# Three modulation vectors of layer 0 as rows on TensorE, and all 31 convolution taps of layer 0 on VectorE

## The chip, the cores and the metric

The kernel runs on one core of one Trainium2 chip. The metric is the device time of one execution in microseconds (us). One execution was taken by the profiler, and all rows shown here come from it. PE is TensorE (matmuls), DVE is VectorE, ACT is ScalarE, POOL is GpSimd, and SP is the engine that issues most of the DMAs. SPq, ACTq and POOLq are the sequencers that issue DMAs.

## What is computed

Two streams of 256 tokens of width 1024, `ctx` and `x`, go through two layers of a first block; then `x` alone goes through a second block. Only the first layer is touched by the change. Cut to what matters there (both streams run it, each with its own modulation vector):

```python
mod = split(silu(c) @ w_mod[l] + b_mod[l], 6)        # x;  the same weights with silu(c_ctx) for ctx
shift1, scale1, gate1, shift2, scale2, gate2 = mod   # parts 0, 1, 2, 3, 4, 5, each 1024 long
xn = rms_norm(x, g1) * (1 + scale1) + shift1
p = xn @ w_in                                        # q, k, v, fourier, conv, pool columns
attn = attend(q, k, v)
four = fft2(p_f).real @ w_f
glu = p_c[:256] * sigmoid(p_c[256:])
y = depthwise_conv(glu, dw_w, width 31) + dw_b       # 256 channels
conv = silu(layer_norm(y)) @ w_pw
mix = concat(attn, four, conv, pool) @ w_out
x = x + gate1 * mix
xn = rms_norm(x, g2) * (1 + scale2) + shift2
x = x + gate2 * swiglu(xn)
```

Part 2 is therefore needed after `@ w_out`, parts 3 and 4 at the second norm, part 5 at the end of the layer.

## The kernel before

Activations are kept feature by token: 128 features on the partitions, 512 columns, of which 256 belong to each stream (`x` is s=0, `ctx` is s=1). A large product is split into three products of rounded high and low halves (`mm3` at L270, `tm` at L283): a weight half of 512 KB is loaded by SP into the ring `raw` of 4, ACT writes its high part `wh` (L241) and DVE, seldom POOL, the low part `wl` (L243). The ring of `wh`, `wl` also has 4 buffers.

The program's text is written as generators on `Flow` (L114), a small clock of estimated times: `tick` advances it with each product, `spawn` starts a side job, `yield d` gives up for d estimated us, and `join` waits for a job. This only sets in which order instructions are written. The order on PE, DVE, ACT and POOL is then made by a scheduler; each engine runs its own list strictly in that order. SP's list is as written.

**Startup** (L479 to L485, `LOADS = "mhmhmm"`). SP loads `XC` (the input, four times 512 KB), then in turn weights of modulation (`m`, `mod_pair`) and of the first projection (`h`). `mod_pair(g)` (L437) makes a quarter of parts 0 and 1 of layer 0 on PE. silu(c) of both streams lies in `scf` as 32 columns (2 used) for each of 8 blocks k of 128 inputs. The array is used as four groups of 32 columns: for each k four matmuls with the same small weights `scf[:, k]` and four different sets of 128 weight columns write four groups of 32 partitions of one PSUM tile `p_mod`. ACT copies it to SBUF, one transpose on PE (`p_modt`) turns rows to columns, and DVE adds the bias. `in0_k` (L464) then norms block k and issues 12 products of the projection `p_c` (the two convolution halves). At the end `scb_fill` (L367) spreads silu(c) over all partitions by 16 transposes (`p_scb`).

**Side job `mod_bg`** (L390) makes all other modulation vectors, ten parts (those of layer 0 in the order 2, 4, 3, 5). For each block of 128 outputs ACT issues a load of 512 KB into a tile `wm` of four (after a one-column copy on POOL, L398, which ties it to the progress of other work), and DVE multiplies it by the spread silu(c) and sums along the row: once for ctx (L403, result tile `jg`) and once for x (L405, written over `wm`). It begins when both convolutions are written.

**Mixer of layer 0.** After `p_c` come q and k, v (`p_q`, `p_kv`), fourier and pool columns. The convolution of each of two channel tiles f has 31 taps: taps 0 to 7 on PE as products with diagonal matrices (`conv_diag` L551 writes them on ACT, `conv_pe` L559 multiplies into `p_cv`), taps 8 to 30 on DVE as one multiply-add each over 512 columns (`conv_taps`, L567 and L571), then `p_cv` is added (L575). `conv_ln` (L582) follows: mean by PE (`p_mean`), subtraction on DVE (L591), squares on ACT (L593), `p_var`, the root on POOL (`rs_r`, L297), its spread by PE (`p_lnr`), multiplication on DVE (L606), silu on ACT (L607), and the product `p_pw` (L614). Attention runs first for s=1, then for s=0: per unit `p_s` (PE), minimum (DVE), exponential (ACT), transposes (PE), copy `pT` (ACT), `p_o` (PE). The output projection `p_wo` of 512 columns runs over k = 0 to 3 (fourier, pool), 6 and 7 (convolution), 4 and 5 (attention) for m = 0 to 3, then for m = 4 to 7 stream by stream. `update` adds gate1 (part 2) times it to `XC`; then comes the second norm (`norm_mod`), whose normed blocks `AH`, `AL` feed `p_ua`.

Of the kernel before, what the change touches and what calls it, by code (L numbers as in the profile page):

```python
# [24 lines left out]
F32 = mybir.dt.float32  # L25
# [3 lines left out]
OP = mybir.AluOpType  # L29
AX = mybir.AxisListType  # L30

D = 1024
KT = 8
T = 256
NF = 22
EPS = 1e-6
TAPS = 31
# [7 lines left out]
LOADS = "mhmhmm"  # L45
NPE = 8
CVD, FOD = 0.9, 1
# [104 lines left out]
@with_exitstack  # L152
def tile_kernel(ctx, tc, xin, pk_d, rows_d, lc_d, bc_d, wmod0, wmod, win, wout, wfi, wfo, wsm, win2, wproj, wout2,
                wgu, wdn, wst, pos, out, dump=None):
    nc = tc.nc
# [35 lines left out]
    def P(name, i=0, n=1):  # L191
        return pk[:, PK[name] + i:PK[name] + i + n]
# [197 lines left out]
    def mod_bg(parts, *deps):  # L390

        yield from wait(*deps)
        for l, part, with_ctx, gap_ in parts:
# [20 lines left out]
            mods.add((l, part))  # L414

# [83 lines left out]
    for l in range(2):  # L501
# [4 lines left out]
        with ExitStack() as mctx:  # L506
# [40 lines left out]
            def conv_diag(f):  # L547

                w = lpool.tile([128, D], F32, tag="wm", name="cdg", bufs=WMB)
                for j in range(NPE):  # L550
                    S.activation(w[:, 128 * j:128 * j + 128], ident, AF.Copy,  # L551
                                 scale=pk[:, PK[f"dw_{l}"] + f * TAPS + j:PK[f"dw_{l}"] + f * TAPS + j + 1])
                return w

            def conv_pe(f, w):

                cps[f] = psm("p_cv")
                for j in range(NPE):
                    PE.matmul(cps[f][:, :N].rearrange("p (s t) -> p s t", t=T), w[:, 128 * j:128 * j + 128],  # L559
                              GP[:, f, :, j:j + T], start=j == 0, stop=j == NPE - 1)  # L560
                    tick(0.0017 * N)

            def conv_taps(f, delay):
                y = Y[:, f].rearrange("p (s t) -> p s t", t=T)
                dw = PK[f"dw_{l}"] + f * TAPS
                per = 0.35 * ns
                V.tensor_scalar(y, GP[:, f, :, NPE:NPE + T], pk[:, dw + NPE:dw + NPE + 1], P(f"db_{l}", f), op0=OP.mult,  # L567
                                op1=OP.add)
                yield per + delay
                for j in range(NPE + 1, TAPS):  # L570
                    V.scalar_tensor_tensor(y, GP[:, f, :, j:j + T], pk[:, dw + j:dw + j + 1], y, op0=OP.mult, op1=OP.add)  # L571
                    yield per + delay
                while f not in cps:
                    yield 0.3
                V.tensor_tensor(Y[:, f], cps[f][:, :N], Y[:, f], op=OP.add)  # L575
                yield per
                G.tensor_copy(snap, Y[:, f, 0:1])
# [224 lines left out]

            cdg = [conv_diag(f) for f in range(2)]
            if l == 1:
# [21 lines left out]
            if l == 0:  # L826
                spawn(mod_bg([(0, 2, True, BG0), (0, 4, True, BG0), (0, 3, True, BG0), (0, 5, True, BG1),
                              (1, 1, True, BG1), (1, 0, True, BG1), (1, 2, False, BG1), (1, 4, False, BG1),
                              (1, 3, False, BG1), (1, 5, False, BG1)], cv0, cv1))
            for s in streams[::-1]:  # L830
# [15 lines left out]
            done(n_, 3)  # L846
            for f in range(2):
                conv_pe(f, cdg[f])
            at = []
# [535 lines left out]
def _pack(inp):  # L1385
    inp = {k: np.asarray(v) for k, v in inp.items()}
    a = {}
# [64 lines left out]

_ORDER = ["xin", "pk", "rows", "lc", "bc", "wmod0", "wmod", "win", "wout", "wfi", "wfo", "wsm", "win2", "wproj", "wout2",
          "wgu", "wdn", "wst", "pos"]
# [18 lines left out]
```

## Time and profile before

| | |
|---|---|
| median of 3 runs | 1367.46 us (1367.43 to 1368.42) |
| the profiled execution | 1368.16 us, span in the trace 1366.5 us |
| mean granted TensorE clock | 0.994 of full |
| DMA | 223.79 MB, mean 164 GB/s |

The span is the time from the first to the last instruction in the trace; the execution's own time is 1.7 us longer. In rows of instructions the columns are start, duration, engine, line, operation, output<-inputs, shape, number of instructions that follow one another (xN), and in brackets the idle time of that engine before it with what ended it. A matmul leaves two records here where its operands are full 32-bit numbers, so four matmuls of a modulation step are eight records.

### The profile page before, as it was taken

How to read it: one execution, taken by the hardware profiler on the slowest of the kernel's cores; microseconds unless marked ns; L12 is line 12 of the kernel's file. 1: busy time of each engine (PE TensorE's matmuls, PEld its weight loads, DVE VectorE, ACT ScalarE, POOL GpSimd, SP SyncE). 2: the span in 40 equal slices, each digit the busy share in tenths (PEclk: the TensorE clock that was granted, in tenths of full speed). 3: DMA queues.
4: the chain of work that ended last, by engine and by line, in shares of the span. 5: the costliest groups of instructions: out<-in, count | busy, mean ns of one | idle time of the engine just before them, and what ended most of it. 6: DMA issues, size and time to landing. Idle time of an engine off the chain costs nothing.

```text
span 1366.5 us, 23461 instructions
## 1 busy us (share of the span) xinstructions
PE 1329.0 (97%) x9220; PEld 1193.9 (87%) x9220; DVE 893.6 (65%) x1572; ACT 608.3 (45%) x1016; POOL 262.1 (19%) x295
## 2 busy tenths in 40 slices
PE   5999999899999999999999999999999999999997
PEld 3886569788888888899799999999999999999997
DVE  4597998999873333369577666665655657655554
ACT  5434534323232222244655554455655555544452
POOL 1034634143310000123330000110200003222211
PEclk9999999999999999999999999999999999999998
DMA  9424452687973222333145555665335344545463
GB/s 367 181 77 137 141 170 95 230 262 259 318 254 108 93 83 76 105 133 135 47 145 180 185 176 162 193 244 171 108 120 175 109 145 169 192 168 176 157 203 105
DMA packets 66478, 223.79 MB, mean 164 GB/s; under 512 B 7488, under 2 KB 8640, under 8 KB 66368
## 3 DMA queue, kind: packets, MB, share of 16 engines
q1 hardware_dynamic: 53824, 178.16, 38.9%
q10 hardware_dynamic: 12080, 42.50, 9.1%
q8 instruction: 72, 1.18, 0.4%
q0 software_dynamic: 464, 1.64, 0.3%
q14 instruction: 38, 0.31, 0.1%
HBM read 221.22 MB, written 1.05 MB: 163 GB/s over the span
## 4 chain that ended last, share of the span: by engine, by line
PE 90%; DVE 4%; POOL 2%; ACT 1%; DMA 1%; issue 1%; SPq 0%; POOLq 0%; DVEq 0%; ACTq 0%
PE p_dn L271 6%; PE p_dn L273 6%; PE p_dn L272 6%; PE p_ua L272 5%; PE p_ua L273 5%; PE p_ua L271 5%; PE p_ug L272 5%; PE p_ug L273 5%; PE p_ug L271 4%; PE p_wo L271 2%; PE p_wo L272 2%; PE p_wo L273 2%; PE p_bq L287 2%; PE p_bq L289 2%; PE p_bq L288 2%; PE p_ga L273 2%
## 5 line engine op out<-in xcount | busy, mean ns | idle before, releaser
L243 DVE TENSOR_TENSOR wl<-raw,wh 128x1024 fp32r<-128x1024 f32 (+2 forms) x340 | 388.6, 1145 | 279.0 <-ACT wh L241 277.8
L241 ACT CAST wh<-raw 128x1024 fp32r<-128x1024 f32 (+1 forms) x344 | 332.1, 973 | 296.9 <-PE p_dn L272 91.8
L273 PE MATMUL p_dn<-HH,wl 128*128 128x256 f32 (+1 forms) x550 | 171.7, 312 | 0.5 <-DVE wl L243 0.5
L271 PE MATMUL p_dn<-HH,wh 128*128 128x256 f32 (+1 forms) x550 | 172.0, 313 | 0.0
L272 PE MATMUL p_dn<-HL,wh 128*128 128x256 f32 (+1 forms) x550 | 171.6, 312 | 0.0
L313 POOL TENSOR_TENSOR ss<-ss,sq 128x256 f32<-128x256 f32 (+1 forms) x43 | 49.3, 1145 | 438.0 <-ACT sq L312 292.0
L272 PE MATMUL p_ua<-AL,wh 128*128 128x258 f32 (+2 forms) x368 | 122.9, 334 | 3.7 <-DVE AL L339 3.7
L273 PE MATMUL p_ua<-AH,wl 128*128 128x258 f32 (+2 forms) x368 | 122.8, 334 | 0.0
L273 PE MATMUL p_ug<-AH,wl 128*128 128x258 f32 (+2 forms) x368 | 122.3, 332 | 0.0
L271 PE MATMUL p_ua<-AH,wh 128*128 128x258 f32 (+2 forms) x368 | 122.1, 333 | 0.0
L272 PE MATMUL p_ug<-AL,wh 128*128 128x258 f32 (+2 forms) x368 | 122.0, 331 | 0.0
L271 PE MATMUL p_ug<-AH,wh 128*128 128x258 f32 (+2 forms) x368 | 121.6, 331 | 0.0
L273 PEld LDWEIGHTS p_dn<-HH,wl 128*128 128x128 f32 x550 | 104.3, 190 | 6.7 <-DVE wl L243 0.7
L272 PEld LDWEIGHTS p_dn<-HL,wh 128*128 128x128 f32 x550 | 104.3, 190 | 6.1
L271 PEld LDWEIGHTS p_dn<-HH,wh 128*128 128x128 f32 x550 | 104.3, 190 | 6.2 <-ACT wh L241 0.2
L405 DVE SCALAR_TENSOR_TENSOR wm<-wm,scb 128x1024 f32<-128x1024 f32 x80 | 99.0, 1242 | 10.1 <-DMA wm<-in_wmod 9.9
L272 PEld LDWEIGHTS p_ua<-AL,wh 128*128 128x128 f32 x368 | 69.7, 189 | 11.3 <-DVE AL L339 4.1
L273 PEld LDWEIGHTS p_ua<-AH,wl 128*128 128x128 f32 x368 | 69.9, 190 | 7.1
L271 PEld LDWEIGHTS p_ua<-AH,wh 128*128 128x128 f32 x368 | 69.8, 190 | 7.2
L272 PEld LDWEIGHTS p_ug<-AL,wh 128*128 128x128 f32 x368 | 69.5, 189 | 7.2
L273 PEld LDWEIGHTS p_ug<-AH,wl 128*128 128x128 f32 x368 | 69.4, 189 | 6.9
L271 PEld LDWEIGHTS p_ug<-AH,wh 128*128 128x128 f32 x368 | 69.3, 188 | 7.0
(367 smaller groups left out, 3329.4 us busy)
## 6 DMA issues: line engine op xcount, KB each, us to landing
raw<-in_wfi SPq DMA_DIRECT2D x88, 512.0 KB, 3.7
raw<-in_win SPq DMA_DIRECT2D x84, 512.0 KB, 3.9
wm<-in_wmod ACTq DMA_DIRECT2D x80, 512.0 KB, 4.5
raw<-in_wgu SPq DMA_DIRECT2D x44, 512.0 KB, 3.7
raw<-in_wout SPq DMA_DIRECT2D x24, 512.0 KB, 3.6
raw<-in_wfo SPq DMA_DIRECT2D x32, 384.0 KB, 3.1
raw<-in_wfo SPq DMA_DIRECT2D x32, 320.0 KB, 3.2
rawm<-in_wmod SPq DMA_DIRECT2D x16, 512.0 KB, 10.1
```

The costliest lines, as they stand in the source:

```text
L241: S.copy(h[:, :n], raw[:, :n])
L243: (G if every and j % every == 0 else V).tensor_tensor(lo[:, :n], raw[:, :n], h[:, :n].bitcast(F32), op=OP.subtract)
L271: PE.matmul(ps, w[0], a[0], start=first, stop=False, **kw)
L272: PE.matmul(ps, w[0], a[1], start=False, stop=False, **kw)
L273: PE.matmul(ps, w[1], a[0], start=False, stop=last, **kw)
L287: PE.matmul(ps, a[0], w[0], start=k == 0, stop=False)
L288: PE.matmul(ps, a[0], w[1], start=False, stop=False)
L289: PE.matmul(ps, a[1], w[0], start=False, stop=k == KT - 1)
L313: (eng or G).tensor_tensor(ss[0][:, cs], ss[0][:, cs], sq[:, :n], op=OP.add)
L405: V.scalar_tensor_tensor(w, w, 1.0, scb[:, 0], op0=OP.mult, op1=OP.mult, accum_out=modv[:, l, part, 0, k:k + 1])
```

## The change

1. `NPE` becomes a pair `(0, 8)`: layer 0 has no taps on PE. `conv_diag`, `conv_pe`, `p_cv` and the final add are left out there; all 31 taps of both channel tiles run on DVE. Layer 1 stays as it was.
2. Parts 2, 4 and 3 of layer 0 leave `mod_bg`. A new side job `mod_pe` makes them on PE in four column groups as `mod_pair` does, now 256 weight columns for each group: per block n (24 in all, 8 for each part) one load of 512 KB from a new array `wmodr` on ACT's queue, and four matmuls into `p_modr`. After 8 blocks ACT copies the rows (L440), two transposes (`p_modq`) and DVE adds follow.
3. The loads use the four `wm` buffers, run two blocks ahead of the products (`MLAG`), and have no copy on POOL ahead of them. `mod_bg` starts with (0, 5) when the convolutions and `mod_pe` are written.

```diff
-NPE = 8
+NPE = (0, 8)
+MPE = (2, 4, 3)
+MGAP, MLAG = 4.0, 2
...
+    def mod_pe():
+        ws = {}
+        def load(n):
+            if n < 8 * len(MPE):
+                ws[n] = lpool.tile([128, D], F32, tag="wm", name="wmr", bufs=WMB)
+                S.dma_start(ws[n], wmodr[n])
+        for n in range(MLAG):
+            load(n)
+        for i, part in enumerate(MPE):
+            p = psm("p_modr")
+            for k in range(KT):
+                n = 8 * i + k
+                load(n + MLAG)
+                yield MGAP
+                w = ws.pop(n)
+                for c in range(4):
+                    PE.matmul(p[32 * c:32 * c + 32, :256], scf[:, k], w[:, 256 * c:256 * c + 256], start=k == 0,
+                              stop=k == KT - 1)
+            row = wk.tile([128, 512], F32, tag="ev", name="row", bufs=EV)
+            S.copy(row[:, :256], p[:, :256])
+            yield 0.6
+            pt = psm("p_modq")
+            for b in range(2):
+                PE.transpose(pt[:, 128 * b:128 * b + 128], row[:, 128 * b:128 * b + 128], ident)
...
-                for j in range(NPE + 1, TAPS):
+                for j in range(n + 1, TAPS):
                     V.scalar_tensor_tensor(y, GP[:, f, :, j:j + T], ...
-                while f not in cps:
-                    yield 0.3
-                V.tensor_tensor(Y[:, f], cps[f][:, :N], Y[:, f], op=OP.add)
+                if n:
+                    while f not in cps:
+                        yield 0.3
+                    V.tensor_tensor(Y[:, f], cps[f][:, :N], Y[:, f], op=OP.add)
...
-            cdg = [conv_diag(f) for f in range(2)]
+            if NPE[l]:
+                cdg = [conv_diag(f) for f in range(2)]
...
             if l == 0:
-                spawn(mod_bg([(0, 2, True, BG0), (0, 4, True, BG0), (0, 3, True, BG0), (0, 5, True, BG1),
+                mpe = spawn(mod_pe(), 1.0)
+                spawn(mod_bg([(0, 5, True, BG1), ...], cv0, cv1, mpe))
...
-            for f in range(2):
-                conv_pe(f, cdg[f])
+            if NPE[l]:
+                for f in range(2):
+                    conv_pe(f, cdg[f])
```

How the scheduler's lists move is seen at three places. The first is the head of ACT's list at startup; `scf` is silu(c), `cdg` the diagonals, `ss`, `sq` and `ssl` the squares of the first norm, `row<-p_mod` the end of the first `mod_pair`. Before:

```order
L175 DMA pk<-in_pk 128x300
L363 ACT_TABLE_LOAD
L363 ACTIVATE scf<-pk 128x8 x2
L551 ACTIVATE cdg<-ident,pk 128x128 x16
L307 ACTIVATE ss<-XC 128x512
```

The same place after the change:

```order
L177 DMA pk<-in_pk 128x300
L425 DMA wmr<-in_wmodr 128x1024 x2
L365 ACT_TABLE_LOAD
L365 ACTIVATE scf<-pk 128x8 x2
L425 DMA wmr<-in_wmodr 128x1024 x2
L309 ACTIVATE ss<-XC 128x512
```

The first four loads of `mod_pe` stand at the very start of the program, among SP's first loads, since their buffers are free and nothing holds them; the 16 diagonals are gone.

The second place is PE's list at the end of `p_c`, where q begins (`p_scb` are the transposes of `scb_fill`). Before:

```order
L373 MATMUL p_scb<-ident,scf 128x128 x4
L271 MATMUL p_c<-AH,wh 128x512 x4
...
L271 MATMUL p_c<-AH,wh 128x512 x4
...
L287 MATMUL p_q<-wh,AH 128x256
L288 MATMUL p_q<-wl,AH 128x256
```

The same place after the change:

```order
L491 MATMUL p_modt<-ident,row 128x128
L375 MATMUL p_scb<-ident,scf 128x128 x16
L437 MATMUL p_modr<-wmr,scf 32x256 x16
L273 MATMUL p_c<-AH,wh 128x512 x4
...
L273 MATMUL p_c<-AH,wh 128x512 x4
L437 MATMUL p_modr<-wmr,scf 32x256 x4
...
L437 MATMUL p_modr<-wmr,scf 32x256 x12
L289 MATMUL p_q<-wh,AH 128x256
```

Eight of the 24 blocks (32 matmuls, n = 0 to 7) come before the first q product. The four blocks n = 4 to 7 need loads that wait for the first four buffers.

The third place is PE's list at the end of attention (`p_s` are scores and their transposes, `p_o` the attention output). Before, `p_mean` stands inside attention of s=1:

```order
L676 MATMUL p_s<-KTt,QT_573 128x256 x4
L686 MATMUL p_s<-ident,pe 128x128 x4
L587 MATMUL p_mean<-Y,mean_w 128x512 x2
L686 MATMUL p_s<-ident,pe 128x128 x2
L715 MATMUL p_o<-pT,VT 64x128 x4
```

After the change it stands behind the last scores of s=0:

```order
L728 MATMUL p_s<-ident,pe 128x128 x8
L629 MATMUL p_mean<-Y,mean_w 128x512 x2
L757 MATMUL p_o<-pT,VT 64x128 x8
L761 MATMUL p_o<-ident,awd 128x128
L640 MATMUL p_var<-ones,lsq 128x1 x8
L645 MATMUL p_lnr<-ident,rs_r 128x128 x4
L656 MATMUL p_pw<-Y,sm 128x512 x2
L444 MATMUL p_modq<-ident,row 128x128 x2
L437 MATMUL p_modr<-wmr,scf 32x256 x10
L656 MATMUL p_pw<-Y,sm 128x512 x2
L437 MATMUL p_modr<-wmr,scf 32x256 x10
L273 MATMUL p_wo<-AH,wh 128x512 x4
```

The chain of the convolution's layer norm, which had the whole of attention of s=0 beside it, now has only the last `p_o` and, between its two halves of `p_pw`, blocks of `p_modr`. Of the other 16 blocks (n = 8 to 23), 8 stand in six groups inside attention of s=0, and 8 in five groups from here on, the last ahead of the second norm. From layer 1's fourier product on, the lists are the same.

## Rows read from the trace of the kernel before

**Rows 1.** The page, busy time of each engine.

```profile
PE 1329.0 (97%) x9220; PEld 1193.9 (87%) x9220; DVE 893.6 (65%) x1572; ACT 608.3 (45%) x1016; POOL 262.1 (19%) x295
```

**Rows 2.** The page, chain that ended last: shares by engine.

```profile
PE 90%; DVE 4%; POOL 2%; ACT 1%; DMA 1%; issue 1%; SPq 0%; POOLq 0%; DVEq 0%; ACTq 0%
```

**Rows 3.** Windows at startup: stretch, then length, busy PE, PEld, DVE, ACT, POOL, clock, DMA share, GB/s.

```profile
5.00:10.00 5.00, 0.00 (x0) 0.00 (x0) 0.00 (x0) 5.00 (x17) 0.00 (x0) 1.00 0.96 345
35.00:40.00 5.00, 5.00 (x71) 3.94 (x70) 2.35 (x4) 2.02 (x5) 0.00 (x0) 1.00 1.03 410
45.00:50.00 5.00, 4.97 (x34) 3.66 (x27) 3.47 (x6) 1.91 (x4) 0.00 (x0) 1.00 0.01 3
```

**Rows 4.** Timeline of 18 to 29 us, the steps that the first projection waits for.

```profile
18.65 1.04 ACT L241 CAST wh<-raw 128x1024 fp32r<-128x1024 f32 x1 [0.18 <-DMA raw<-in_win]
...
22.07 1.04 POOL L297 TENSOR_TENSOR rs_r<-rs_v,mhalf 128x4 f32<-128x4 f32 x1
...
28.63 1.21 PE L271 MATMUL p_c<-AH,wh 128*128 128x512 f32 x4 [0.77 <-ACT AH L471]
```

**Rows 5.** Timeline of PE, modulation steps of 128 columns, and a neighbour.

```profile
24.21 3.64 PE L446 MATMUL p_mod<-rawm,scf 128*32 128x128 f32 x64
...
34.95 0.40 PE L272 MATMUL p_c<-AL,wh 128*128 128x512 f32 x1
35.18 0.40 PE L273 MATMUL p_c<-AH,wl 128*128 128x512 f32 x1
35.51 1.74 PE L446 MATMUL p_mod<-rawm,scf 128*32 128x128 f32 x56
```

**Rows 6.** DMA issues: tile, queue, count, KB each, median us to landing.

```profile
wm<-in_wmod ACTq DMA_DIRECT2D x80, 512.0 KB, 4.5
```

**Rows 7.** The chain that ended last in 60 to 210 us, its steps of the diagonal products.

```profile
95.01 6.02 PE p_cv L559 x14
...
109.17 6.89 PE p_cv L559 x16
```

**Rows 8.** Groups of DVE by form in 60 to 204 us.

```profile
L571 DVE SCALAR_TENSOR_TENSOR Y<-GP,pk,Y 128x512 f32<-128x512 f32 x44 | 31.4, 752 | 0.0
L403 DVE SCALAR_TENSOR_TENSOR jg<-wm,scb 128x1024 f32<-128x1024 f32 x23 | 30.0, 1303 | 1.1 <-DMA wm<-in_wmod 1.1
L405 DVE SCALAR_TENSOR_TENSOR wm<-wm,scb 128x1024 f32<-128x1024 f32 x22 | 27.4, 1245 | 0.0
```

**Rows 9.** Timeline of PE around the two idle times in the mixer.

```profile
119.58 1.00 PE L686 MATMUL p_s<-ident,pe 128*128 128x128 f32 x4 [1.89 <-ACT pe L682]
...
192.53 1.09 PE L715 MATMUL p_o<-pT,VT 128*64 128x128 f32 x14 [0.31 <-ACT pT L688]
...
195.37 2.08 PE L271 MATMUL p_wo<-AH,wh 128*128 128x512 f32 x4 [1.49 <-ACT AH L727]
```

**Rows 10.** Windows in the mixer, columns as in rows 3.

```profile
120.00:125.00 5.00, 4.98 (x19) 2.41 (x19) 3.61 (x8) 2.21 (x9) 0.18 (x1) 0.66 0.91 306
140.00:160.00 20.00, 19.49 (x85) 10.72 (x84) 20.00 (x35) 13.46 (x30) 15.91 (x14) 1.00 0.41 132
195.00:200.00 5.00, 4.63 (x12) 3.11 (x12) 5.00 (x11) 1.34 (x2) 1.12 (x1) 0.66 0.60 207
```

**Rows 11.** Timeline of the convolution's layer norm, DVE, ACT and POOL.

```profile
124.06 1.28 DVE L591 TENSOR_TENSOR Y<-Y,p_mean 128x512 f32<-128x512 f32 x2 [0.27 <-PE p_mean L587]
...
125.78 1.15 ACT L593 ACTIVATE lsq<-Y 128x512 f32<-128x512 f32 x2
...
139.45 1.93 POOL L297 TENSOR_TENSOR rs_r<-rs_v,mhalf 128x4 f32<-128x4 f32 x1
...
146.94 1.28 ACT L607 ACT_TABLE_LOAD   x1
148.23 1.52 ACT L607 ACTIVATE Y<-Y,pk 128x512 f32<-128x512 f32 x2
```

**Rows 12.** Timeline of PE at the second norm.

```profile
252.00 0.38 PE L272 MATMUL p_ua<-AL,wh 128*128 128x256 f32 x1 [2.13 <-DVE AL L339]
```

More of the change, by code (lines that the diff above doesn't have):

```diff
@@ L152, in tile_kernel @@
 @with_exitstack
-def tile_kernel(ctx, tc, xin, pk_d, rows_d, lc_d, bc_d, wmod0, wmod, win, wout, wfi, wfo, wsm, win2, wproj, wout2,
-                wgu, wdn, wst, pos, out, dump=None):
+def tile_kernel(ctx, tc, xin, pk_d, rows_d, lc_d, bc_d, wmod0, wmodr, wmod, win, wout, wfi, wfo, wsm, win2, wproj,
+                wout2, wgu, wdn, wst, pos, out, dump=None):
     nc = tc.nc
@@ L414, in mod_bg @@
             mods.add((l, part))
+    def mod_pe():
[22 more added lines that the diff above has]
+                PE.transpose(pt[:, 128 * b:128 * b + 128], row[:, 128 * b:128 * b + 128], ident)
+            yield 0.5
+            v = pt[:, :256].rearrange("p (b c x) -> p x c b", b=2, x=32)
+            for s in range(2):
+                d = modv[:, 0, part, s]
+                V.tensor_tensor(d.rearrange("p (c b) -> p c b", b=2), v[:, s],
+                                P("bmod0", part * 8, 8).rearrange("p (c b) -> p c b", b=2), op=OP.add)
+                if part == 4:
+                    V.scalar_tensor_tensor(d, d, 1.0, P("g2_0", 0, 8), op0=OP.add, op1=OP.mult)
+            yield 0.4
+            mods.add((0, part))
     sctx = ctx.enter_context(ExitStack())
@@ L549, in conv_diag @@
                 w = lpool.tile([128, D], F32, tag="wm", name="cdg", bufs=WMB)
-                for j in range(NPE):
+                for j in range(NPE[l]):
                     S.activation(w[:, 128 * j:128 * j + 128], ident, AF.Copy,
@@ L557, in conv_pe @@
                 cps[f] = psm("p_cv")
-                for j in range(NPE):
+                for j in range(NPE[l]):
                     PE.matmul(cps[f][:, :N].rearrange("p (s t) -> p s t", t=T), w[:, 128 * j:128 * j + 128],
-                              GP[:, f, :, j:j + T], start=j == 0, stop=j == NPE - 1)
+                              GP[:, f, :, j:j + T], start=j == 0, stop=j == NPE[l] - 1)
                     tick(0.0017 * N)
@@ L566, in conv_taps @@
                 per = 0.35 * ns
[L567 removed]
+                n = NPE[l]
+                V.tensor_scalar(y, GP[:, f, :, n:n + T], pk[:, dw + n:dw + n + 1], P(f"db_{l}", f), op0=OP.mult,
                                 op1=OP.add)
                 yield per + delay
[L570 removed]
+                for j in range(n + 1, TAPS):
                     V.scalar_tensor_tensor(y, GP[:, f, :, j:j + T], pk[:, dw + j:dw + j + 1], y, op0=OP.mult, op1=OP.add)
                     yield per + delay
[L573 to L576 removed]
+                if n:
+                    while f not in cps:
+                        yield 0.3
+                    V.tensor_tensor(Y[:, f], cps[f][:, :N], Y[:, f], op=OP.add)
+                    yield per
                 G.tensor_copy(snap, Y[:, f, 0:1])
@@ L826, in tile_kernel @@
             if l == 0:
-                spawn(mod_bg([(0, 2, True, BG0), (0, 4, True, BG0), (0, 3, True, BG0), (0, 5, True, BG1),
-                              (1, 1, True, BG1), (1, 0, True, BG1), (1, 2, False, BG1), (1, 4, False, BG1),
-                              (1, 3, False, BG1), (1, 5, False, BG1)], cv0, cv1))
+                mpe = spawn(mod_pe(), 1.0)
+                spawn(mod_bg([(0, 5, True, BG1), (1, 1, True, BG1), (1, 0, True, BG1), (1, 2, False, BG1), (1, 4, False, BG1),
+                              (1, 3, False, BG1), (1, 5, False, BG1)], cv0, cv1, mpe))
             for s in streams[::-1]:
@@ L1416, in _pack @@
     a["wmod0"] = inp["w_mod"][0][:, :2048].reshape(4, 2, 128, 2, 4, 256).transpose(4, 0, 2, 1, 3, 5).reshape(4, 4, 128, 1024)
+    a["wmodr"] = np.concatenate([inp["w_mod"][0][:, 1024 * i:1024 * i + 1024].reshape(8, 128, 1024) for i in MPE])
     a["wmod"] = inp["w_mod"].transpose(0, 2, 1).reshape(2, 48, 128, 1024)
@@ L1450, in _pack @@
     return {k: np.ascontiguousarray(v) for k, v in a.items()}
-_ORDER = ["xin", "pk", "rows", "lc", "bc", "wmod0", "wmod", "win", "wout", "wfi", "wfo", "wsm", "win2", "wproj", "wout2",
+_ORDER = ["xin", "pk", "rows", "lc", "bc", "wmod0", "wmodr", "wmod", "win", "wout", "wfi", "wfo", "wsm", "win2", "wproj", "wout2",
           "wgu", "wdn", "wst", "pos"]
```

## The prediction

> **What bounds the kernel now.** I read the page first. PE is busy for 97% of the span [rows 1], and the chain that ended last is 90% PE and 4% DVE [rows 2]. So a stage is worth what it costs PE, either in work or in waits, and DVE's time counts only where PE waits for it. Then I read the stages that the change touches. The first is startup. From 5 to 40 us the DMA engines are full (share 0.96 to 1.03, 345 to 410 GB/s), and by 45 us they are still [rows 3]. The reader is to see there that data sets the pace until the first projection runs: a weight cast that waited for its DMA starts at 18.65, the root of the first norm follows it on POOL at 22.07, and the first product `p_c` comes at 28.63 [rows 4]. From then on PE runs nearly without a gap. The second stage is the mixer, 60 to 200 us. PE is full there but for 1.89 us before 119.58 and 1.49 us before 195.37 [rows 9]; behind each lies a stretch of 5 us with a granted clock of 0.66 [rows 10]. DVE is full too: 20.00 of 20 us in 140 to 160 [rows 10].
>
> 0.2% is about what a measurement of this kernel can tell from no change; that is 2.7 us.
>
> **The sum** is made against the profiled execution, 1368.16 us, which lies 0.7 above the median.
>
> *1. Loads at startup.* The first four `wmr` loads now head ACT's list, so 4 x 512 KB = 2.1 MB enter a stretch in which the DMA engines are full. At 410 GB/s [rows 3] that is 5.1 us. The stretch 5 to 10 us ran at 345 GB/s and so had room for at most 65 GB/s x 5 us = 0.33 MB, or 0.8 us. The data that the first projection waits for comes later by 4.3 to 5.1 us; I take **+4.7**. The 16 diagonals that leave ACT there lie beside the loading (ACT's 5.00 busy us of 5 to 10 [rows 3]) and are worth nothing. By the Trainium skill (DMA: Bandwidth & Descriptors, "Issuing engines are not separate DMA queues") transfers issued on several engines run on the same 16 DMA engines and interleave; by that ACT's queue gives these loads no bandwidth of their own, which agrees with the full share, and the sum stays as it is.
>
> *2. Eight modulation steps before q.* A step of 128 columns is eight records: 1.74 us for 56 records is 0.25 us a step [rows 5]. With 256 columns I take twice that, 0.5. Eight steps stand before the first `p_q`, where PE is full: **+4.0**. Below, the step costs no more for 256 columns than for 128 (2.0); above, it has the pace of the slow row at 24.21, 3.64 us for 64 records, or 0.455 a step [rows 5], which doubled is 0.91 (7.3 in all).
>
> *3. Waits for n = 4 to 7.* These loads wait until steps 0 to 3 have read their buffers. A load of 512 KB takes 4.5 us to land [rows 6], while between the steps stand 16 and 8 products of `p_c` at 0.23 us (34.95 to 35.18 [rows 5]), 3.7 and 1.8 us. The first is late by about 0.8; the others share the DMA engines with SP's weights for q. **+1.5**, between 0 and 3. While PE waits, q's products are queued behind it.
>
> *4. The diagonal products leave.* 16 matmuls of 512 columns, two records each. The chain holds 6.02 us for 14 and 6.89 for 16 [rows 7], 0.43 a record, so 32 x 0.43 = **-13.8**. They are on the chain, and PE is full around them. DVE gets 16 taps at 0.75 in their place (12 us) and loses 24 pairs at 2.55 (61 us) [rows 8]; being off PE's path, this counts nothing by itself.
>
> *5. The other 16 steps.* 16 x 0.5 = 8.0. Three pairs of transposes `p_modq`: four transposes took 1.00 us [rows 9], so 0.5 a pair, 1.5. Changing between full tiles and column groups: p_c at 34.95 and 35.18 are 0.23 apart, and the `p_mod` after it comes 0.33 later [rows 5]; that is 0.1 a change, 0.2 in and out, and 14 groups give 2.8. Of the eight steps inside attention I let four lie where PE would have waited for an exponential: -2.0 (between 0 and -4.0). Together **+10.3**. The Trainium skill (TensorEngine Tiling (Array Packing), "Key Properties") says that changing the tiling mode drains TensorE, which speaks against steps scattered in 14 groups. The 0.1 us agrees with a short drain; were it nothing, this part would be 7.5.
>
> *6. The idle times go.* At both places other PE work now stands (steps; the convolution's part of `p_wo`). 1.89 + 1.49 [rows 9], and the two stretches at 0.66, each 5 x 0.34 = 1.7 us [rows 10]: **-6.8**. Bounds are -6.8 and -3.4, should the low clock come at another place.
>
> *7. The end of the convolution is uncovered.* This is the new wait. `p_mean` moves behind the last scores, since DVE's 62 taps end later in its list. After it come, one behind the other, subtraction 1.28 and the second square 0.58, the root on POOL (1.04 in rows 4, 1.93 in rows 11; I take 1.5), the first multiplication (0.64, as one of the subtractions), ACT's table load 1.28 and the first silu 0.76 [rows 11]. That is 6.0 us. Beside it lies only the last `p_o`, 1.09 + 0.3 [rows 9]. 4.7 us are left, and an idle of that length is likely to be followed by a stretch at the lower clock, as both idle times above are: 1.7 more. **+6.4**, between 2 (steps of `p_modr` and weights' products fill more of it) and 10 (the last tap comes later than the last scores). All of `p_wo` is queued behind it.
>
> *8. The second norm.* PE waits 2.13 us for DVE's `AL` [rows 12]. The pairs of part 5 stand a little differently between these rows of DVE: **+0.5**, from -2.1 (the wait goes) to +2.5 (one pair more ahead).
>
> Sum: 4.7 + 4.0 + 1.5 - 13.8 + 10.3 - 6.8 + 6.4 + 0.5 = **+6.8**, so 1375.0 in the profiled execution's terms and **1374.3** as a median. In a word: PE's work stays nearly the same (24 steps with their transposes and changes for 16 products), and what is added is the data at startup.
>
> **Rivals.**
>
> *Faster: DVE's list was what paced the mixer.* DVE is full in 140 to 160 us, and a score unit's minimum can stand behind a pair of 2.55 us [rows 8, 10]. Without the pairs each of the eight units of s=0 comes, say, half of one row sooner (0.6 us, together -5.0); the taps end before attention of s=0 does, so the end of the convolution is covered again (-6.4), and all eight inner steps and their six changes lie in waits (-2.0 and -1.2). 1374.3 - 14.6 = 1359.7. For it speaks that row of DVE; against it that PE is busy for 19.49 us in the same stretch, and the place of `p_mean` in PE's list. It decides if `p_mean` starts before the scores of s=0 are through. Chance 0.20, with partial cases down to a gain of 2.7 us.
>
> *No change: a step of 256 columns costs 0.25, as one of 128 does*, or data at startup is not what the first projection waits for. 24 x 0.25 = 6.0 less: 1368.3. For it speaks that a small step may be bound by its four weight loads rather than its columns; against it the two paces within rows 5, which are both of 128 columns and differ by 1.8, so that something beside a fixed cost sets them. Chance 0.20.
>
> *Slower still: all steps run at the slow pace of rows 5*, 0.91 each, 24 x 0.41 = 9.8 more: 1384.1. That would be so if each step, cut off from the next by other tiles, pays what the row at 24.21 pays. Chance 0.12.
>
> The forecast keeps 0.48. The range from 1361 to 1384 holds it, the rival without change and most of the faster one; left out are the best case of the latter and the slow steps. Faster by over 0.2%: 0.20. Within: 0.20. Slower: 0.48 + 0.12 = 0.60. The slower cases hold most of the chance; their own range is 1370.5 to 1384.
>
> **What would show it.** Right: the first `p_c` at about 33 us instead of 28.63, and the first `p_q` some 10 us later than before; rows of `p_modr` of eight records with 0.5 us a step; no `p_cv` in layer 0; `p_mean` after the last scores, then a gap of PE of 4 to 5 us that ends with ACT's silu, and the clock at 0.66 behind it; nothing else than a shift from layer 0's feed-forward part on. Wrong, if the first `p_c` stays within 1 us of 28.63 (then the loads collide with nothing), if a step takes 0.25 or 0.9, if `p_mean` starts while scores still run, or if no gap follows it.

## The result, and the profile after

The changed kernel takes 1384.7 us (median of 4 runs, 1381.4 to 1386.6) against 1367.9 of the kernel before: ratio 1.0118, interval 1.0093 to 1.0143, so 13 to 20 us slower. The forecast was slower, 1374.3, with a range up to 1384. The direction was right; the forecast 6.8 us are less than half of what was measured. The profiled execution of the change takes 1382.96 us with a span of 1380.5, 14.0 more than the span before.

Where the 14.0 us lie is read from a few landmarks of PE's timeline. Each number is the start or the end of a tile's products in the two traces.

| landmark on PE | before | after | difference | of it new in this stage |
|---|---|---|---|---|
| first `p_c` | 28.63 | 32.40 | +3.8 | +3.8 |
| first `p_q` | 59.77 | 67.74 | +8.0 | +4.2 |
| last `p_o` ends | 193.88 | 181.40 | -12.5 | -20.5 |
| last 512-wide `p_wo` ends | 200.08 | 209.90 | +9.8 | +22.3 |
| first 512-wide `p_ua` | 253.04 | 265.31 | +12.3 | +2.5 |
| first `p_dn` of layer 0 | 354.90 | 365.58 | +10.7 | -1.6 |
| end of the span | 1366.5 | 1380.5 | +14.0 | +3.3 |

`p_dn` is the last product of the feed-forward part. The rows `p_ua` and `p_dn` belong together: a stretch of lower clock behind the wait at the second norm lies behind the first wide `p_ua` before the change and ahead of it afterwards, so the second norm and what follows are 0.9 us longer in all.

PE's busy time on the page grows by 3.7 us, little, as it should when 24 steps replace 16 products [rows 1]; DVE has 41 us less:

```profile
PE 1332.7 (97%) x9386; PEld 1196.1 (87%) x9386; DVE 852.6 (62%) x1498; ACT 602.4 (44%) x1001; POOL 224.9 (16%) x261
```

So most of the time is not in work but in when PE gets it. The timeline of PE of the change shows each place. First startup and the steps ahead of q, which answer to [rows 4] and [rows 5]:

```profile
32.40 1.20 PE L273 MATMUL p_c<-AH,wh 128*128 128x512 f32 x4 [0.77 <-ACT AH L511]
...
55.07 0.27 PE L491 MATMUL p_modt<-ident,row 128*128 128x128 f32 x1
55.18 1.91 PE L375 MATMUL p_scb<-ident,scf 128*128 128x128 f32 x16
57.02 1.93 PE L437 MATMUL p_modr<-wmr,scf 128*32 128x256 f32 x32
...
67.17 0.64 PE L437 MATMUL p_modr<-wmr,scf 128*32 128x256 f32 x8 [0.59 <-DMA wmr<-in_wmodr]
67.74 0.39 PE L289 MATMUL p_q<-wh,AH 128*128 128x256 f32 x1
```

The reader is to see that a step costs what was forecast (32 records are four steps in 1.93 us, 0.48 each), that of the waits for later loads only 0.59 us came, and that the start itself is 3.8 us late. The windows say why: 417 GB/s already in 5 to 10 us, where it was 345 [rows 3].

```profile
5.00:10.00 5.00, 0.00 (x0) 0.00 (x0) 0.85 (x2) 1.96 (x4) 0.00 (x0) 1.00 1.02 417
```

Then the middle of the mixer. The two old idle times [rows 9] are gone, but there are new ones:

```profile
122.34 1.13 PE L784 MATMUL p_fa<-lc,U 128*128 128x256 f32 x4 [0.88 <-DVE U L805]
125.00 1.10 PE L838 MATMUL p_pl<-S,sm 128*128 128x512 f32 x2 [1.09 <-issue]
127.84 0.55 PE L704 MATMUL p_qt<-ident,qt 128*128 128x128 f32 x3 [0.18 <-DVE qt L699]
134.08 0.33 PE L761 MATMUL p_o<-ident,awd 128*128 128x128 f32 x1 [3.37 <-ACT awd L760]
```

Together 5.5 us. The longest is put down to ACT; the timeline of DVE and POOL around it shows who was late:

```profile
125.02 1.40 DVE L612 SCALAR_TENSOR_TENSOR Y<-GP,pk,Y 128x512 f32<-128x512 f32 x2
...
128.81 1.94 POOL L827 TENSOR_TENSOR S<-S 128x530 f32<-128x530 f32 x1
129.73 3.23 DVE L612 SCALAR_TENSOR_TENSOR Y<-GP,pk,Y 128x512 f32<-128x512 f32 x2
130.82 1.59 POOL L828 TENSOR_TENSOR S<-S 64x514 f32<-64x514 f32 x1
132.49 2.95 POOL L831 TENSOR_TENSOR S<-S,lc 64x512 f32<-64x512 f32 x2
132.89 0.74 DVE L582 SCALAR_TENSOR_TENSOR AL<-p_pl,pk,AH 128x512 fp32r<-128x512 f32 x1
133.55 0.15 DVE L753 RECIPROCAL asum<-asum 128x2 f32<-128x2 f32 x1
...
133.73 0.30 ACT L760 COPY awd<-asum 128x128 f32<-128x128 f32 x1 [3.87 <-DVE asum L753]
134.40 1.59 DVE L612 SCALAR_TENSOR_TENSOR Y<-GP,pk,Y 128x512 f32<-128x512 f32 x1
```

A reciprocal of 0.15 us, for which ACT and then PE wait, stands in DVE's list behind two taps, and these two take 3.23 us beside POOL's pool mixer, where the two at 125.02, which hardly meet its sums, take 1.40. A stretch of lower clock follows, and further on the uncovered end of the convolution, which was forecast:

```profile
135.00:140.00 5.00, 5.00 (x9) 1.69 (x7) 5.00 (x10) 2.27 (x8) 2.04 (x2) 0.69 0.01 3
185.00:190.00 5.00, 1.61 (x5) 0.91 (x6) 1.28 (x2) 2.80 (x3) 0.36 (x1) 0.59 0.00 0
190.00:195.00 5.00, 5.00 (x28) 2.06 (x27) 0.44 (x4) 0.00 (x0) 0.00 (x0) 0.73 0.06 18
...
615.00:620.00 5.00, 5.00 (x28) 5.00 (x27) 3.82 (x10) 1.42 (x3) 0.00 (x0) 0.56 0.37 146
```

```profile
178.15 1.97 PE L629 MATMUL p_mean<-Y,mean_w 128*128 128x512 f32 x4
...
181.63 0.38 PE L640 MATMUL p_var<-ones,lsq 128*128 128x1 f32 x2 [0.23 <-ACT lsq L635]
182.34 1.72 PE L640 MATMUL p_var<-ones,lsq 128*128 128x1 f32 x14 [0.33 <-ACT lsq L635]
185.42 0.70 PE L645 MATMUL p_lnr<-ident,rs_r 128*128 128x128 f32 x4 [1.35 <-POOL rs_r L299]
189.09 3.77 PE L656 MATMUL p_pw<-Y,sm 128*128 128x512 f32 x4 [2.96 <-ACT Y L649]
...
193.00 1.49 PE L437 MATMUL p_modr<-wmr,scf 128*32 128x256 f32 x20
194.43 1.98 PE L656 MATMUL p_pw<-Y,sm 128*128 128x512 f32 x4
...
261.55 0.58 PE L274 MATMUL p_ua<-AL,wh 128*128 128x256 f32 x1 [4.04 <-DVE AL L341]
```

After the last `p_o` PE is idle for 0.23 + 0.33 + 1.35 + 2.96 = 4.9 us, and the same four records of `p_pw` take 3.77 us at the low clock and 1.98 at full: 1.8 more. The last row answers to [rows 12]: the wait at the second norm is 4.0 us where it was 3.7 in two pieces (1.55 and the 2.13 of [rows 12]). The window at 615 us shows one more stretch at 0.56, and the one ahead of it is at 0.76. They come behind an idle of 1.4 us that the kernel before has as well, without such a stretch in its profile. Before the change, then after it:

```profile
600.79 0.74 PE L271 MATMUL p_c<-AH,wh 128*128 128x256 f32 x4 [1.35 <-ACT AH L338]
```

```profile
611.47 0.74 PE L273 MATMUL p_c<-AH,wh 128*128 128x256 f32 x4 [1.35 <-ACT AH L340]
```

From layer 1's first `p_c` to its first `p_q` the change takes 16.73 us, and `mod_only` below, which has the same idle and no lower clock behind it, takes 13.87: the stretch costs some 2.9 us. It was met in some of the profiled executions below and not in others. Single runs of one kernel lie up to 8 us apart; how much of that is this stretch is not shown.

### The profile page after: what moved, and what is told of

It reads as the page before. It is cut to its first block, busy times and chain, and to the rows that moved or that the text cites. A ratio compares the mean times of both kernels' runs of the same rounds, so it can differ in the third digit from the quotient of the medians.

```text
span 1380.5 us, 23662 instructions
## 1 busy us (share of the span) xinstructions
PE 1332.7 (97%) x9386; PEld 1196.1 (87%) x9386; DVE 852.6 (62%) x1498; ACT 602.4 (44%) x1001; POOL 224.9 (16%) x261
## 4 chain that ended last, share of the span: by engine, by line
PE 90%; DVE 4%; DMA 2%; ACT 2%; issue 1%; POOL 1%; POOLq 0%; DVEq 0%; ACTq 0%; SPq 0%
PE p_dn L273 6%; PE p_dn L275 6%; PE p_dn L274 6%; PE p_ua L274 5%; PE p_ua L275 5%; PE p_ug L274 5%; PE p_ug L275 4%; PE p_ua L273 4%; PE p_ug L273 4%; PE p_wo L274 2%; PE p_wo L273 2%; PE p_wo L275 2%; PE p_bq L289 2%; PE p_bq L290 2%; PE p_bq L291 2%; PE p_ga L275 2%
## 5 line engine op out<-in xcount | busy, mean ns | idle before, releaser
L407 DVE SCALAR_TENSOR_TENSOR wm<-wm,scb 128x1024 f32<-128x1024 f32 x56 | 68.1, 1219 | 10.2 <-DMA wm<-in_wmod 10.0
```

Source lines behind the costliest of these rows:

```text
L407: V.scalar_tensor_tensor(w, w, 1.0, scb[:, 0], op0=OP.mult, op1=OP.mult, accum_out=modv[:, l, part, 0, k:k + 1])
```

## The experiments

**Theory A** after the result: the loss has four places, the loads at startup, the eight steps ahead of q, the wait on DVE's taps in the mixer, and the uncovered end of the convolution. **Theory B**, the rival: the modulation steps on PE, scattered in 14 groups with their changes of column groups, are the loss, and the taps on DVE are free, as the forecast had assumed. Ratios are to runs of the kernel before on the same chips (medians 1369.1 to 1370.5).

**Each half of the change alone.** `conv_only` keeps `NPE = (0, 8)` and takes `mod_pe` away:

```diff
-                mpe = spawn(mod_pe(), 1.0)
-                spawn(mod_bg([(0, 5, True, BG1), ...], cv0, cv1, mpe))
+                spawn(mod_bg([(0, 2, True, BG0), (0, 4, True, BG0), (0, 3, True, BG0), (0, 5, True, BG1), ...], cv0, cv1))
```

> All taps on DVE in layer 0, but parts 2, 4, 3 made by the DVE pairs as before. Theory A (the loss of the change lies in the mixer: DVE's 62 taps stand ahead of rows that PE waits for, and the end of the convolution is uncovered): no loads at startup, first p_q within 1 us of 59.8; -13.8 for the diagonal products, -3.4 for the old idle times, +7 for a new wait on DVE at about 115 to 130 us, +7 for the end of the convolution; 1362 to 1368, more if gate 1 comes late because 61 us of pairs now follow the taps. Theory B (the modulation steps on PE and their changes of column groups are the loss, the taps on DVE cost nothing): 1350 to 1356, no idle of PE above 1 us before the last scores.

Measured 1376.7 (ratio 1.0057, interval 1.0037 to 1.0078). The wait on DVE is there without any step on PE:

```profile
116.16 1.10 PE L784 MATMUL p_fa<-lc,U 128*128 128x256 f32 x4 [1.22 <-DVE U L805]
118.35 1.10 PE L838 MATMUL p_pl<-S,sm 128*128 128x512 f32 x2 [0.65 <-issue]
123.02 0.55 PE L704 MATMUL p_qt<-ident,qt 128*128 128x128 f32 x3 [1.78 <-DVE qt L699]
127.38 1.22 PE L718 MATMUL p_s<-KTt,QT 64*128 64x256 f32 x2 [2.10 <-ACT pT L730]
```

That is 5.75 us, about as much as in the change (5.5), and B falls. First `p_q` comes at 61.05, and from there to the end of the last 512-wide `p_wo` it takes 139.6 us against 140.3 before: of the 13.8 us of diagonal products that have left PE, 0.7 are seen. The rest went into this wait, the lower clock behind it and the end of the convolution, where 3.95 and 2.03 us of idle stand. The time is above A's 1362 to 1368 for the reason that its expectation named: the 24 pairs now follow 62 taps on DVE, and PE waits 1.8, 3.8 and 3.5 us ahead of the second norm. `mod_only` is the other half:

```diff
-NPE = (0, 8)
+NPE = (8, 8)
```

> Parts 2, 4, 3 on PE as in the change, taps 0 to 7 still diagonal products on PE. Theory A: startup +2 to +4, 24 steps of 0.57 = 13.7, the two old idle times and half-clock stretches partly filled (-3 to -7): 1376 to 1382, p_mean inside attention of s=1 and no idle of PE over 2 us in 110 to 200 us. Theory B: it carries all of the change's loss without the gain of the diagonal products: 1384.7 + 13.8 = about 1398.

Measured 1385.9 (1.0123, 1.0108 to 1.0138), between the two, nearer to A. First `p_q` at 66.2, and from there to the last `p_o` 140.8 us, 6.7 more than before. Some 16 steps stand there; they come to 9.1 us at 0.57 each, so most of their price is paid on PE; the pairs that they replace bring nothing that outweighs it. Neither half of the change gains: alone they cost 7 and 16 us, together 17.

**Loads and early steps.** `late_loads` holds the first four loads back until the last block of the first norm is written:

```diff
                 ws[n] = lpool.tile([128, D], F32, tag="wm", name="wmr", bufs=WMB)
+                if n < WMB:
+                    G.tensor_copy(ws[n][:, 0:1], AL[:, KT - 1, 0:1].bitcast(F32))
                 S.dma_start(ws[n], wmodr[n])
```

> The change, with a one-column copy on POOL from the last normed block ahead of each of the first four loads of mod_pe, so that they cannot be issued at startup. If the startup loads cost what the trace of the change shows (first p_c 3.8 us later), first p_c is back at 28.4 to 29, and the steps move behind p_q: 1377 to 1381. If the early loads cost nothing in the end (PE is full until q anyway), 1383 to 1387.

Measured 1372.6 (1.0019, 1.0010 to 1.0029): 12 us of the 17 come back, more than expected. First `p_c` is at 28.17 and first `p_q` at 58.67, 9.1 earlier than in the change, and the first step stands at 64.8, beside q. The wait on DVE also shrinks, from 5.5 to 2.0 us:

```profile
125.51 0.70 PE L720 MATMUL p_s<-KTt,QT 64*128 64x256 f32 x2 [0.94 <-DVE awo L768]
127.29 5.37 PE L814 MATMUL p_fw<-U,sm 128*128 128x512 f32 x8 [1.08 <-DVE U L807]
...
175.63 0.80 PE L647 MATMUL p_lnr<-ident,rs_r 128*128 128x128 f32 x4 [1.35 <-POOL rs_r L299]
179.40 3.67 PE L658 MATMUL p_pw<-Y,sm 128*128 128x512 f32 x4 [2.97 <-ACT Y L651]
```

The taps' input comes sooner too: the first tap starts at 59.37 instead of 68.40. The steps, now behind `p_q`, stand where PE would otherwise reach the rows of DVE sooner; that this is why the wait is shorter is not shown by itself. The taps are as slow as in the change (mean 826 ns in 60 to 150 us, there 830). `steps_late` keeps the loads early and moves the steps, which it also writes a little closer together:

```diff
-MGAP, MLAG = 4.0, 2
+MGAP, MLAG = 3.2, 2
...
         for n in range(MLAG):
             load(n)
+        yield 16.0
```

> The change with its four loads still at startup, but the first step of mod_pe written later, so that all 24 steps stand behind the q products. It divides the 9 us that the late loads brought. If loads and early steps each have a part (3.8 for the loads, 4.8 for the eight steps and their wait): first p_c stays at 32.4, first p_q at 63 to 64 instead of 67.7, and the steps lie in waits of PE later: 1378 to 1381. If the loads alone cause it: first p_q at 67 or later, 1383 to 1386.

Measured 1383.2 (1.0114, 1.0094 to 1.0133). First `p_q` comes at 64.73, nearly as expected, but that brings nothing: DVE keeps PE waiting 5.35 us before `p_fw`, followed by clocks of 0.58 and 0.74. `early_dummies` puts the loads alone into the kernel before, four loads that nobody reads, at the same places of ACT's list:

```diff
+    for i in range(4):
+        dmy = (lpool if i < 2 else spool).tile([128, D], F32, ...)
+        S.dma_start(dmy, wmod[0, 16 + i])
```

> The kernel before with four loads of 512 KB, which nobody reads, at the places on ACT's list where the change has its first four loads; all else as before. If the loads alone delay the startup: first p_c at 32 to 33 instead of 28.6, first p_q at 63 to 64 instead of 59.8, and the time 3 to 5 us above the kernel before: 1372 to 1375. If the later stages make up for it: 1369 to 1371.

Measured 1377.2 (1.0058, 1.0040 to 1.0075): 6.7 us, not 4. First `p_c` is at 32.72 as expected, but first `p_q` at 67.02, 7.25 late.

```profile
56.83 0.27 PE L455 MATMUL p_modt<-ident,row 128*128 128x128 f32 x1
60.71 1.20 PE L271 MATMUL p_c<-AH,wh 128*128 128x512 f32 x4 [1.86 <-ACT AH L475]
...
67.02 0.39 PE L287 MATMUL p_q<-wh,AH 128*128 128x256 f32 x1 [0.45 <-ACT sg L626]
```

The scheduler, whose plan now holds these loads, writes 24 products of `p_c` between the last `p_mod` and the last `p_modt` where before it wrote 16. So fewer products are left to cover the chain from there to the last normed blocks, and PE waits 1.86 us for it. In the change, which has the same order, the first four steps lie in just that wait (57.02 above). Of the 8.0 us by which q is late there, the loads alone bring 7.25.

`no_steps` was meant to price the steps, by leaving out the matmuls of 21 of 24:

```diff
-                for c in range(4):
+                for c in range(4 if k == 0 else 0):
```

> The change with the matmuls of only one of each eight modulation steps (21 of 24 steps are left out, their loads stay): the price of the steps on PE. 21 x 0.57 = 12.0 if all lie on PE's path: 1372 to 1374. If those inside attention lie in waits of PE and the wait on DVE grows where they filled it: 6 to 9 less, 1376 to 1379.

Measured 1389.1 (1.0143, 1.0124 to 1.0163): a miss, and a dose of the other term. Without steps nothing held the buffers of the loads, so 19 of the 24 were issued before 83 us, where the change has 12. First `p_c` came at 37.16 and first `p_q` at 82.12. From there to the first 512-wide `p_ua` it took 190.7 us, 6.8 less than the change's 197.6, for 14 steps left out behind q: some 0.5 each, if nothing else made the difference.

**The wait on DVE.** `taps46` leaves out the last 8 taps of each tile and keeps the written order:

```diff
                 for j in range(n + 1, TAPS):
+                    if l == 0 and j >= TAPS - 8:
+                        yield per + delay
+                        continue
```

> The change without the last 8 of the 31 taps of each channel tile of layer 0 (that part of the convolution is left out), the written order of everything else kept: DVE has as many taps there as in the kernel before. If the 16 added taps, standing ahead of rows of DVE that PE waits for, cause the wait of PE at 122 to 134 us (5.5 us) and the lower clock behind it (1.6): both go, the end of the convolution stays uncovered because p_mean keeps its place on PE: 1376 to 1379. If the wait has another cause (rows of POOL, order on ACT): 1382 to 1386.

Measured 1374.5 (1.0039, 1.0025 to 1.0052). One wait of 1.11 us is left between 110 and 142 us, no lower clock there, and from first `p_q` to last `p_o` it takes 107.4 us instead of 113.7. `no_pool` leaves the window sums of the pool mixer of layer 0 out, so that POOL has one copy for each tile in their place:

```diff
+                if l == 1:
                     ...
+                else:
+                    G.tensor_copy(PY, UP[:, :, POOL_PAD:POOL_PAD + T])
+                    return
```

> The change with the pool mixer of layer 0 left out on POOL (one copy per channel tile in place of 7 to 10 operations, the pool window means are not computed). Taps that ran beside POOL's operations took 1.0 us and more, others 0.72. If that is contention between DVE and POOL, all taps now take 0.72 to 0.75, the taps end 3 to 5 us sooner, and PE's wait at 122 to 134 us falls to 2 to 4: 1378 to 1382. If the taps are slow for another reason, they stay above 0.9 in the same stretch, 1383 to 1386.

Measured 1373.9 (1.0036, 1.0022 to 1.0049), more than expected. No wait of PE over 0.3 us is left between 100 and 165 us, and the groups of DVE in 60 to 150 us show the taps and the weights' low parts quicker, the change first, `no_pool` second:

```profile
L612 DVE SCALAR_TENSOR_TENSOR Y<-GP,pk,Y 128x512 f32<-128x512 f32 x60 | 47.7, 830 | 0.0
L245 DVE TENSOR_TENSOR wl<-raw,wh 128x1024 fp32r<-128x1024 f32 x10 | 14.3, 1427 | 7.0 <-ACT wh L243 7.0
```

```profile
L612 DVE SCALAR_TENSOR_TENSOR Y<-GP,pk,Y 128x512 f32<-128x512 f32 x60 | 42.8, 748 | 0.0
L245 DVE TENSOR_TENSOR wl<-raw,wh 128x1024 fp32r<-128x1024 f32 x11 | 13.4, 1220 | 8.1 <-ACT wh L243 7.5 <-PE p_wo L275 0.5
```

The 1.09 us ahead of `p_pl`, for which the change's trace shows no cause, are gone as well; what of `no_pool`'s gain is quicker taps and what is the absence of POOL's sums is not told apart. The kernel before had its taps on DVE until about 110 us and its pool sums on POOL from 109.5 to 116 and from 142 to 154; with 62 taps the two overlap. By the Trainium skill (SBUF — State Buffer, "Who interferes with whom") a DVE instruction with two inputs in SBUF contends with a GpSimd instruction that reads SBUF; a tap has two such inputs. The traces agree for the pool sums: 3.23 us for two taps beside them, 1.40 without. Not every POOL instruction does it: two taps that start at 88.37 in the change, beside POOL's root of 128x12 (87.39 to 90.04, by the profile's rough spans), take 1.40 too.

**The end of the convolution.** `taps_early` writes the taps closer together, so that `p_mean` comes ahead of the scores of s=0:

```diff
-            cv0 = spawn(conv_taps(0, CVD))
-            cv1 = spawn(conv_taps(1, CVD), 0.5)
+            cv0 = spawn(conv_taps(0, CVD if l else 0.5))
+            cv1 = spawn(conv_taps(1, CVD if l else 0.5), 0.5)
```

> The change, with the taps of layer 0 written closer together (estimated gap 0.5 instead of 0.9), which puts p_mean before the scores of s=0. If the uncovered end of the convolution costs 6.7 us (4.9 of idle before p_pw and 1.8 of half clock behind it), this goes: -6.7; but the taps stand closer ahead of the fourier, pool and attention rows on DVE, so the wait on DVE before 135 us grows from 5.5 to between 6 and 10: 1378 to 1384. If DVE's order does not matter (theory B), 1383 to 1387.

Measured 1381.9 (1.0090, 1.0075 to 1.0105). `p_mean` is at 158.9, but `p_pw` only at 186 and still with a wait of 1.9; the waits on DVE are 2.2, 1.5 and 2.5 us. `late_swap` takes `late_loads` and turns the halves of the sum round in layer 0:

```diff
-            join(cv)
+            la, lb = ((4, 6), (6, 8)) if l == 0 else ((6, 8), (4, 6))
+            join(atw if l == 0 else cv)
             for m in range(4):
-                wo_mm(ps4[m][:, :N], m, range(6, 8), cs, 5)
+                wo_mm(ps4[m][:, :N], m, range(*la), cs, lb[1] - 1)
```

> The change with late loads, and in layer 0 the attention half (k = 4, 5) of the 512-wide p_wo ahead of the convolution half (k = 6, 7), the last product of which now ends the sum. If the uncovered end of the convolution costs 6.7 us (4.9 idle between the last p_o and p_pw, 1.8 of half clock), the 24 products of 0.23 = 5.5 us now lie there: idle under 1.5 us, no stretch below 0.9 there, 1366 to 1369. If the end of the convolution is not what PE waits for, 1371 to 1374.

Measured 1373.3 (1.0031, 1.0019 to 1.0043): no gain on `late_loads`. The scheduler put 12 of the 24 products between `p_var` and `p_lnr`, none between `p_lnr` and `p_pw`, and there the wait stayed:

```profile
185.88 1.98 PE L658 MATMUL p_pw<-Y,sm 128*128 128x512 f32 x4 [2.97 <-ACT Y L651]
```

**The second norm**, where most versions wait 3.6 to 4.1 us for `AL` rows behind pairs of part 5. `before_hold` is the kernel before with one edit:

```diff
-            while (l, part) == (0, 5) and not ffn:
+            while (l, part) == (0, 5) and len(ffn) < 4:
```

> The kernel before, in which mod_bg holds the DVE pairs of part 5 of layer 0 until four feed-forward tiles are written instead of one. If these pairs, standing ahead of AL rows, cause the 3.7 us of idle and the 1.7 us of lower clock at the second norm (248 to 260 us): 1363 to 1366. If DVE is late there for another reason: 1367 to 1371.

Measured 1366.2 (0.9982, 0.9970 to 0.9993), at the edge of the expected range. The wait is gone and the clock there stays at 1.00, as its windows show; of the 4.1 us that the first 512-wide `p_ua` comes sooner, 2.5 to 3 are left in the median.

```profile
245.00:250.00 5.00, 5.00 (x40) 4.82 (x39) 2.07 (x4) 2.95 (x5) 0.00 (x0) 1.00 0.34 108
250.00:255.00 5.00, 5.00 (x24) 4.03 (x23) 2.82 (x5) 1.60 (x4) 1.90 (x4) 1.00 0.88 295
```

**Put together.** `late_swap_hold` has the late loads, the swap and the held pairs.

> Late loads, the swapped order of p_wo and the held pairs together. The change of the study has 4.0 us of idle at the second norm where the kernel before has 3.7; the three add up if they are independent: 1361 to 1365. If the held pairs only move the wait on, 1366 to 1369.

Measured 1366.7 (0.9986, 0.9973 to 0.9998). The wait at the second norm is gone here too and has not moved on (the first 512-wide `p_ua` comes 3.9 us sooner than in `late_swap`); what is missing from the sum is the swap, which brought nothing. `late_hold_early_taps` has the early taps in place of the swap.

> The change with late loads, with the pairs of part 5 held back, and with the taps of layer 0 written closer together (0.5), which puts p_mean and p_pw before the last units of attention. With late loads the steps stand beside q, k, v, where the taps begin earlier, so the taps' earlier place should cost less than it did with early loads. If the uncovered end of 6.7 us goes and the wait on DVE grows by 1 to 3: 1360 to 1364, ahead of the kernel before by 5 or more. If the wait on DVE takes it back as with early loads: 1365 to 1368.

Measured 1369.3 (0.9998, 0.9989 to 1.0007), a miss: `p_pw` at 173 us still waits 1.9 us with a clock of 0.50 behind it, and DVE's waits grow to 1.4 in a further place. `late_covered_end` has `late_swap_hold`'s edits and longer estimates in the layer norm of layer 0, which move `p_pw` back in PE's list:

```diff
                 r = rsqrt(p[:, :2 * ns], 2 * ns, 1.0 / 256, True)
-                yield 2.0
+                yield 4.0 if l == 0 else 2.0
...
                     S.activation(Y[:, f], Y[:, f], AF.Silu, bias=P(f"lb_{l}", f), scale=P(f"lg_{l}", f))
-                yield 0.8
+                yield 11.0 if l == 0 else 0.8
```

> Late loads, swapped p_wo and held pairs, and in layer 0 p_pw written later behind the silu, so that PE's list has four modulation steps (2.3 us) between p_lnr and the first p_pw and all 12 products of one k between p_var and p_lnr. If the uncovered end of the convolution costs what the trace of the change shows, the wait of 3.0 us before p_pw falls below 1 and the clock behind it stays above 0.9: 1361 to 1364, 3 to 5 ahead of the run without this. If the wait only moves, 1365 to 1368.

Measured 1361.5 (0.9947, 0.9928 to 0.9965): 5.2 us ahead of `late_swap_hold`, which ran on another chip, and the fastest of all kernels here, 23 us ahead of the change and 4.7 ahead of `before_hold`. The wait before `p_pw` falls from 3.0 to 1.35, not below 1. The clock behind it is 1.00 in 185 to 190 us, as expected, where `late_swap_hold` has 0.66; ahead of `p_pw` the low clock stays, as it does there. First `late_swap_hold`, then three windows of `late_covered_end`:

```profile
185.00:190.00 5.00, 3.65 (x6) 1.54 (x6) 0.00 (x0) 1.99 (x3) 0.00 (x0) 0.66 0.00 0
```

```profile
175.00:180.00 5.00, 4.67 (x22) 4.11 (x22) 0.66 (x3) 0.87 (x3) 1.02 (x1) 0.66 0.00 0
180.00:185.00 5.00, 5.00 (x37) 3.62 (x40) 1.29 (x4) 0.05 (x1) 0.00 (x0) 0.65 0.00 0
185.00:190.00 5.00, 3.65 (x23) 1.62 (x16) 0.35 (x4) 2.76 (x4) 0.00 (x0) 1.00 0.79 275
```

In the two traces the first 512-wide `p_ua` comes 3.6 us sooner (247.76 against 251.34), which is nearly what 1.6 us of idle and 5 x 0.34 = 1.7 of lower clock come to. The profiled execution is the slowest of the six (1365.6 us); from 595 to 605 us it has the stretch of lower clock that was met at 615 in the change. The edit lengthens two estimates at once, and they were not tried apart.

## Why the prediction was right or wrong, step by step

*1. Loads at startup, +4.7.* The mechanism is right, the cost was half as much again. First `p_c` is 3.8 us late (4.1 with the dummies), but q is 7.25 late by the loads alone. The second part is the lost cover of the last norm blocks. It stood in the order shown ahead of the prediction (all 16 `p_scb` behind the last `p_modt`, followed at once by steps) and was not read as a wait.

*2 and 3. Eight steps +4.0 and waits for their loads +1.5.* The step's price holds, 0.48 in a row and 0.57 with changes (1.43 us for 2.5 steps from 193.00 to 194.43). But four of the eight lie in the wait of point 1, and the waits came to 0.59. Points 1 to 3 were 10.2 in all and measured 8.0.

*4. The diagonal products, -13.8; "being off PE's path, this counts nothing by itself".* **This is the step that failed.** 61 us less of pairs does not outweigh 12 us more of taps, for the pairs stood later in DVE's list, and the taps stand ahead of the fourier, attention and pool rows that PE waits for at 122 to 134 us. The price is 5.5 us of idle and 1.6 of lower clock (5 x 0.31). `taps46` leaves 1.1 us of it and `no_pool` no wait above 0.3, so it took the added taps and POOL's sums together. `conv_only` has the same wait with no step on PE. The rival that was forecast on DVE's side had it the other way, that DVE's relief would shorten attention. Whether that happened is not shown: first `p_q` to last `p_o` is 20.5 us shorter, but some 13.8 of it are the diagonal products and some of it has only moved behind the last `p_o`, and `conv_only`, which keeps the pairs and has no steps there, takes nearly the same time (113.0 us, the change 113.7). `p_mean` did not start before the scores were through, which is the sign that this rival had named.

*5. Sixteen steps +10.3.* 16 x 0.57 = 9.1 with their changes, and 1.2 for the transposes `p_modq` (0.4 a pair; the forecast's 0.5 was read at a lower clock), 10.3 before any deduction where the forecast had 12.3. How many of the steps in attention lie in waits is not shown for the change itself. The drain at a change of column groups stays at about 0.1 us and decides nothing; B falls here as well.

*6. Idle times go, -6.8.* The two named ones went; the new ones of point 4 stand in their stead, so PE's idle in the mixer did not become less.

*7. The end of the convolution, +6.4.* Right: 4.9 of idle and 1.8 of low clock, 6.7. `late_covered_end`, which fills half of its last wait, shows that it is paid for: 3.6 us in the traces, 5.2 between the medians. One detail was wrong: the taps end at 147 us, and `p_mean` starts at 178 since its place in PE's list, not DVE, holds it.

*8. The second norm, +0.5.* Near: +0.9 from the last wide `p_wo` to the first `p_dn`, with some two steps and a pair of transposes that stand there. `before_hold` shows that the wait itself is due to the pairs of part 5.

What no term had is the stretch of lower clock at 610 to 620 us, some 2.9 us in the profiled execution. The sum of what was measured is 8.0 to q, +1.8 to the last wide `p_wo` (forecast with points 4 to 7: -3.9), 0.9 to the feed-forward part's `p_dn`, and 3.3 behind it: 14.0, against 6.8. The largest gap, 5.7, is the wait on DVE less what the other terms were better. The upper bound of 1384 was missed by 0.7 because a new wait on DVE was a bound of no term. The rival with slow steps named nearly the measured time, 1384.1, but by luck: the steps took 0.48 and not 0.91. The signs that the prediction had named as right came, or nearly, but for the last one, that nothing but a shift follows; none of them looked at the taps' place in DVE's list.

What stays open is how far `no_pool` gains by quicker taps and how far by POOL's sums being absent, and why the clock falls behind the idle at 610 us in some executions alone.

## What to carry to other kernels

When work is moved on to an engine that is off the critical path, its total matters less than the place in its list: ask which short rows stand behind it, who waits for them, and which other engine slows the moved work at that time. A load that nothing holds back goes to the very start of the program, where it competes with the first data and also shifts the scheduler's plan; a one-column copy ahead of each of four loads, which ties them to later data, was worth 12 us here. And a wait that a change uncovers is best looked for in the engine's list as the stretch without other work between two dependent rows: four small steps put into the right gap were worth 3.6 us in the traces and 5 in the medians, while 24 products put beside it were worth nothing.

## What was not expected of the hardware

Two taps took 3.23 us beside the pool sums on POOL and 1.40 without, and the mean of 60 taps was 830 ns, against 748 in `no_pool`. A wait of 1.4 us at the same place of the program was followed by a stretch at the lower clock in some executions and not in others: a granted clock of 0.76 and 0.56 in 610 to 620 us of the change, 1.00 throughout in `mod_only`.
